# Splitting the first load by partitions and shortening the rows of the last loads in a nearest-neighbour upsampling kernel

## The chip, the cores and the metric

The kernel runs on one core of one Trainium2 chip. The metric is the device time of one execution, in microseconds (us), lower is better. A kernel was run several times, in rounds that alternate with the kernel before on the same chip. A span is the profiled part of one execution; it is about 1.8 us shorter than the time.

The work is done by DVE (VectorE) and ACT (ScalarE), which copy and replicate, and by the core's 16 DMA engines (16 packets are in flight at a time in the trace), which move data between HBM and the on-chip memory SBUF (tiles of 128 partitions). SP (SyncE) only issues the DMAs.

## The reference

```python
def setup_inputs():
    batch, channels, h, w = (16, 64, 64, 64)
    return {'x': np.random.randn(batch, channels, h, w).astype(np.float32), 'scale_factor': 2}

def reference(x, scale_factor):
    ...
    for i in range(new_h):          # 128
        for j in range(new_w):      # 128
            result[:, :, i, j] = x[:, :, i // scale_factor, j // scale_factor].copy()
    return result.astype(np.float32)
```

Every input value is written four times: 16.78 MB in, 67.11 MB out. There is no arithmetic.

## The kernel before

The rows of the input (65,536 rows of 64 values) are cut into eight loads of 2 MB. A load gives each of the 128 partitions 64 neighbouring rows, 16 KB in one piece. All eight are issued at once; the first is moved ahead of the barrier that ends the program's preamble. Then, for every half of a load, DVE replicates 18 rows of 32 and ACT the other 14 into a buffer `u` of 32 KB per partition, and a 4 MB store writes it out. There are two `u` buffers, so two stores can be in flight.

```python
def begin_before_barrier(nc):
    ...
    load = next(i for i in body.instructions if i.engine == sp)
    ...                                   # taken out of the body, put before SP's drain

    blocks = [64, 64, 64, 64, 64, 64, 64, 64]
    K = 32
    KV = 18
    ...
    upool = ctx.enter_context(tc.tile_pool(name="uexp", bufs=2))
    for n, k in enumerate(blocks):
        xt = xpool.tile([P, k, W], fdt, name=f"x{n}")
        nc.sync.dma_start(out=xt[:, :, :], in_=of_block(xf, first, k))
        ...
    for xt, first, k in loaded:
        for r0 in range(0, k, K):
            u = upool.tile([P, K, s, W, s], fdt, name="u")
            nc.vector.tensor_copy(out=u[:, :KV], in_=expanded(xt[:, r0 : r0 + KV, :]))
            nc.scalar.copy(out=u[:, KV:], in_=expanded(xt[:, r0 + KV : r0 + K, :]))
            nc.sync.dma_start(
                out=of_block(of, first, k)[:, r0 : r0 + K, :], in_=u[:, :, :, :, :])
```

Of the kernel before, what the change touches and what calls it, by code (L numbers as in the profile page):

```python
# [1 line left out]

# [4 lines left out]


def begin_before_barrier(nc):



    blocks = nc.main_func.blocks
    main, body = blocks[0], blocks[1]
    sp = mybir.EngineType.SP
    load = next(i for i in body.instructions if i.engine == sp)
    assert isinstance(load, mybir.InstDMACopy), type(load)
    assert not (load.sync_info and load.sync_info.on_wait)
    body.instructions = [i for i in body.instructions if i is not load]
    kept = list(main.instructions)  # L20
    at = next(
        n
        for n, i in enumerate(kept)
        if i.engine == sp and isinstance(i, mybir.InstDrain)
    )
    kept.insert(at, load)
    main.instructions = kept


@with_exitstack  # L30
def kernel(
    ctx: ExitStack,
    tc: tile.TileContext,
    x: bass.AP,
    scale_factor: int,
    out: bass.AP,
):
    nc = tc.nc
    nc.at_finalize(begin_before_barrier)
    P = nc.NUM_PARTITIONS  # L40
    s = int(scale_factor)
    B, C, H, W = x.shape
    R = B * C * H
    fdt = x.dtype



    blocks = [64, 64, 64, 64, 64, 64, 64, 64]

    K = 32  # L50
    assert P * sum(blocks) == R

    KV = 18

    xf = x.rearrange("b c h w -> (b c h) w")
    of = out.rearrange("b c (h hd) w -> (b c h) (hd w)", hd=s)

    def of_block(rows, first, k):
        return rows[first : first + P * k, :].rearrange("(p k) w -> p k w", p=P)

    xpool = ctx.enter_context(tc.tile_pool(name="xin", bufs=1))
    upool = ctx.enter_context(tc.tile_pool(name="uexp", bufs=2))

    loaded = []
    first = 0
    for n, k in enumerate(blocks):
        xt = xpool.tile([P, k, W], fdt, name=f"x{n}")
        nc.sync.dma_start(out=xt[:, :, :], in_=of_block(xf, first, k))
        loaded.append((xt, first, k))
        first += P * k  # L70

    def expanded(rows):
        return rows.unsqueeze(2).unsqueeze(4).to_broadcast(
            [P, rows.shape[1], s, W, s]
        )

    for xt, first, k in loaded:
        for r0 in range(0, k, K):
            u = upool.tile([P, K, s, W, s], fdt, name="u")
            nc.vector.tensor_copy(  # L80
                out=u[:, :KV], in_=expanded(xt[:, r0 : r0 + KV, :])
            )
            nc.scalar.copy(  # L83
                out=u[:, KV:], in_=expanded(xt[:, r0 + KV : r0 + K, :])
            )
            nc.sync.dma_start(
                out=of_block(of, first, k)[:, r0 : r0 + K, :],
                in_=u[:, :, :, :, :],
            )


# [1 line left out]
_INS = ['x', 'scale_factor']  # L93
_OUTS = [((16, 64, 128, 128), 'float32')]

_NUMBERS = {'scale_factor': 2}


# [26 lines left out]
```

## Time and profile before

| | before |
|---|---|
| time, median of 3 (range) | 199.86 us (199.73 to 199.90) |
| span | 198.0 us |
| busy: DMA queue, ACT, DVE | 99.0%, 26%, 21% |
| first data packet starts, after the first issue | 1.02 us |
| last data packet ends | 196.85 us |
| a 16 KB load packet, a 32 KB store packet | 611 ns, 1213 ns |

The last three rows are from the single DMA records of the trace, of which the views below are sums. One packet is one partition's piece of one DMA: 8 loads and 16 stores on 128 partitions leave 3072 data packets.

The page of the profile of the kernel before, its parts 1, 2 and 4. In part 2 the span is cut into 40 slices; "DMA" is the busy share in tenths, "GB/s" what was moved.

```profile
span 198.0 us, 149 instructions
...
DVE 40.9 (21%) x16; ACT 52.0 (26%) x17; POOL 0.2 (0%) x4
...
DMA  8999999999999999999999999999999999999995
GB/s 268 434 434 434 430 427 430 424 427 424 424 424 437 444 463 430 437 430 430 424 424 424 424 437 444 457 437 430 437 430 424 424 424 424 437 437 463 437 430 232
...
DMA 77%; ACT 14%; issue 0%; ACTq 0%
```

The DMA row is full from the second slice to the last but one, at 424 to 463 GB/s. The kernel is bound by the DMA engines. The ACT copies in the chain of part 4 are no second limit: while ACT and DVE fill one `u`, the other `u`'s store keeps the DMA engines busy (99.0% of the span).

The windows view of the same kernel, which the change is to alter: for each stretch its length, the busy time (and instructions) of DVE, ACT and POOL, the clock, the DMA share and GB/s. A packet is counted whole in the stretch where it starts, so a share can pass 1.

```profile
0.00:1.00 1.00, 0.00 (x0) 0.21 (x1) 0.20 (x4) 1.00 0.00 0
1.00:2.00 1.00, 0.00 (x0) 1.00 (x1) 0.00 (x0) 1.00 1.53 295
2.00:4.00 2.00, 0.00 (x0) 0.07 (x1) 0.00 (x0) 1.00 0.82 336
4.00:6.00 2.00, 0.00 (x0) 0.00 (x0) 0.00 (x0) 1.00 0.96 410
6.00:8.00 2.00, 0.15 (x1) 0.15 (x1) 0.00 (x0) 1.00 1.00 426
8.00:10.00 2.00, 2.00 (x1) 2.00 (x1) 0.00 (x0) 1.00 1.05 451
```

Nothing moves in the first microsecond, then the rate climbs, and from 4 us on it is 410 to 451 GB/s. This head is what the change goes for.

The waits view of the same kernel: who waited for what, in total us, times, longest us.

```profile
DVE u L80 <- DMA out_dram<-u: 131.8, 14, 39.3
...
DVE u L80 <- DMA x<-in_x_dram: 7.8, 1, 7.8
```

The second line gives the moment when the first 2 MB have landed: 7.8 us. It is not on the critical path (the first stores are issued at 11.1 and 14.1 us and then stand behind the other loads until about 40 us).

### The profile page before, as it was taken

To read this page: it belongs to the slowest core of one execution; us is meant where nothing else is said; L and a number is where in the kernel's file an instruction comes from. 1 tells how busy PE (TensorE), PEld (TensorE's weight loads), DVE (VectorE), ACT (ScalarE), POOL (GpSimd) and SP (SyncE) were. 2 spreads that over 40 slices of the span, in tenths; PEclk is the share of its full clock that TensorE was granted. 3 is DMA by queue.
4 is the path that set the end of the run, shared out by engine and by line. 5 is a ranking of instruction groups with operands and counts; after the bars stand their busy time and mean duration, and the time that the engine had idled before them with its cause. 6 is when DMAs were issued, how large, how long until landed. Compare 5 with 4: busy or idle time off the path is not lost.

```text
span 198.0 us, 149 instructions
## 1 busy us (share of the span) xinstructions
DVE 40.9 (21%) x16; ACT 52.0 (26%) x17; POOL 0.2 (0%) x4
## 2 busy tenths in 40 slices
DVE  0460000000405050505050505050505050504000
ACT  2480000000415150606060606060606060605000
POOL 0000000000000000000000000000000000000000
DMA  8999999999999999999999999999999999999995
GB/s 268 434 434 434 430 427 430 424 427 424 424 424 437 444 463 430 437 430 430 424 424 424 424 437 444 457 437 430 437 430 424 424 424 424 437 437 463 437 430 232
DMA packets 3456, 83.89 MB, mean 424 GB/s; under 512 B 384, under 2 KB 384, under 8 KB 384
## 3 DMA queue, kind: packets, MB, share of 16 engines
q1 hardware_dynamic: 3456, 83.89, 99.0%
HBM read 16.78 MB, written 67.11 MB: 424 GB/s over the span
## 4 chain that ended last, share of the span: by engine, by line
DMA 77%; ACT 14%; issue 0%; ACTq 0%
DMA out_dram<-u 73%; ACT u L83 14%; DMA x<-in_x_dram 4%; ACTq L83 0%
## 5 line engine op out<-in xcount | busy, mean ns | idle before, releaser
L83 ACT COPY u<-x 128x3584 f32<-128x3584 f32 x16 | 50.8, 3179 | 128.3 <-DMA out_dram<-u 122.5
L80 DVE COPY u<-x 128x4608 f32<-128x4608 f32 x16 | 40.9, 2560 | 139.7 <-DMA out_dram<-u 131.8
L83 ACT ACT_TABLE_LOAD x1 | 1.3, 1283 | 0.8 <-PEq L106 0.8
L106 POOL MEMSET const-bfloat16-1.0<- 128x1 bf16 x1 | 0.1, 102 | 0.0
L106 POOL MEMSET const-uint8-127<- 128x1 uint8 x1 | 0.1, 102 | 0.0
L106 POOL MEMSET const-float32-0.0<- 128x1 f32 x1 | 0.1, 98 | 0.2 <-issue 0.2
L106 POOL MEMSET const-float32-1.0<- 128x1 f32 x1 | 0.1, 98 | 0.0
## 6 DMA issues: line engine op xcount, KB each, us to landing
out_dram<-u SPq DMA_DIRECT2D x16, 4096.0 KB, 16.1
x<-in_x_dram SPq DMA_DIRECT2D x8, 2048.0 KB, 22.9
```

The source lines that it names most:

```text
L80: nc.vector.tensor_copy(out=u[:, :KV], in_=expanded(xt[:, r0 : r0 + KV, :]))
L83: nc.scalar.copy(out=u[:, KV:], in_=expanded(xt[:, r0 + KV : r0 + K, :]))
L106: nc = _bacc.Bacc("TRN2", target_bir_lowering=False, num_devices=1)
```

## The change

The intent, as the diff suggests: let the DMA engines start sooner by issuing first a small load with one packet for each of the 16 engines, issue the rest of the first load behind it before the barrier as well, keep the number of loads at eight by making one load of 4 MB, and use shorter rows (8 KB) where the loads end and the stores begin.

```diff
+EARLY = 2
...
-    load = next(i for i in body.instructions if i.engine == sp)
+    loads = [i for i in body.instructions if i.engine == sp][:EARLY]
...
-    blocks = [64, 64, 64, 64, 64, 64, 64, 64]
+    blocks = [(1, 64), (1, 64), (1, 128), (1, 64), (1, 64), (2, 32), (2, 32)]
...
-    for n, k in enumerate(blocks):
-        xt = xpool.tile([P, k, W], fdt, name=f"x{n}")
-        nc.sync.dma_start(out=xt[:, :, :], in_=of_block(xf, first, k))
+    for n, (j, m) in enumerate(blocks):
+        xt = xpool.tile([P, j, m, W], fdt, name=f"x{n}")
+        src = xf[first : first + j * P * m, :].rearrange(
+            "(j p m) w -> p j (m w)", j=j, p=P
+        )
+
+        for lo, hi in ((0, 16), (16, P)) if n == 0 else ((0, P),):
+            nc.sync.dma_start(out=xt[lo:hi], in_=src[lo:hi])
+        for jj in range(j):
+            parts.append((xt[:, jj], first + jj * P * m, m))
...
```

Copies and stores are the same, except that the last four stores each write 4 MB without gaps.

More of the change, by code (lines that the diff above doesn't have):

```diff
@@ L15, in begin_before_barrier @@
     sp = mybir.EngineType.SP
-    load = next(i for i in body.instructions if i.engine == sp)
-    assert isinstance(load, mybir.InstDMACopy), type(load)
-    assert not (load.sync_info and load.sync_info.on_wait)
-    body.instructions = [i for i in body.instructions if i is not load]
+    loads = [i for i in body.instructions if i.engine == sp][:EARLY]
+    for load in loads:
+        assert isinstance(load, mybir.InstDMACopy), type(load)
+        assert not (load.sync_info and load.sync_info.on_wait)
+    names = [i.name for i in loads]
+    body.instructions = [i for i in body.instructions if i.name not in names]
     kept = list(main.instructions)
@@ L25, in begin_before_barrier @@
     )
-    kept.insert(at, load)
+    kept[at:at] = loads
     main.instructions = kept
@@ L44 @@
     fdt = x.dtype
-    blocks = [64, 64, 64, 64, 64, 64, 64, 64]
+    blocks = [(1, 64), (1, 64), (1, 128), (1, 64), (1, 64), (2, 32), (2, 32)]
     K = 32
-    assert P * sum(blocks) == R
+    assert P * sum(j * m for j, m in blocks) == R
     KV = 18
@@ L56 @@
     of = out.rearrange("b c (h hd) w -> (b c h) (hd w)", hd=s)
-    def of_block(rows, first, k):
-        return rows[first : first + P * k, :].rearrange("(p k) w -> p k w", p=P)
     xpool = ctx.enter_context(tc.tile_pool(name="xin", bufs=1))
     upool = ctx.enter_context(tc.tile_pool(name="uexp", bufs=2))
-    loaded = []
+    parts = []
     first = 0
-    for n, k in enumerate(blocks):
-        xt = xpool.tile([P, k, W], fdt, name=f"x{n}")
-        nc.sync.dma_start(out=xt[:, :, :], in_=of_block(xf, first, k))
-        loaded.append((xt, first, k))
-        first += P * k
+    for n, (j, m) in enumerate(blocks):
[7 more added lines that the diff above has]
+            parts.append((xt[:, jj], first + jj * P * m, m))
+        first += j * P * m
     def expanded(rows):
@@ L75, in expanded @@
         )
-    for xt, first, k in loaded:
-        for r0 in range(0, k, K):
+    for xp, first, m in parts:
+        dst = of[first : first + P * m, :].rearrange("(p m) w -> p m w", p=P)
+        for r0 in range(0, m, K):
             u = upool.tile([P, K, s, W, s], fdt, name="u")
             nc.vector.tensor_copy(
-                out=u[:, :KV], in_=expanded(xt[:, r0 : r0 + KV, :])
+                out=u[:, :KV], in_=expanded(xp[:, r0 : r0 + KV, :])
             )
             nc.scalar.copy(
-                out=u[:, KV:], in_=expanded(xt[:, r0 + KV : r0 + K, :])
+                out=u[:, KV:], in_=expanded(xp[:, r0 + KV : r0 + K, :])
             )
             nc.sync.dma_start(
-                out=of_block(of, first, k)[:, r0 : r0 + K, :],
-                in_=u[:, :, :, :, :],
+                out=dst[:, r0 : r0 + K, :], in_=u[:, :, :, :, :]
             )
```

## The prediction

What it came to: 200.0 us, 80% range 199.2 to 202.8, where before took 199.86. It weighs a gain of 0.2 to 0.5 us (first packet 0.25 us earlier, 0.1 to 0.2 us given back where loads meet stores, 0.07 us for more packets taken off) against a loss of 1 to 4 us from the first load's split. Where a cut is marked, terms and conditions are gone: how the loss would come about, what the first packets would then take, and on what the earlier start depended. The 1 to 4 us and the 0.75 us are estimates.

> **What bounds the kernel now.** The DMA engines. The page has them 99.0% busy over the span of 198.0 us, moving 83.89 MB at 424 GB/s; DVE is busy 21%, ACT 26%. In the trace's DMA records the first data packet starts 1.02 us after the first issue and the last ends at 196.85 us; between them 16 packets are in flight, so there is no hole. A 16 KB load packet takes 611 ns, a 32 KB store packet 1213 ns. Chained end to start, packets form 16 streams of 192 packets and 5.24 MB. 128 x 1213 + 64 x 611 ns is 194.4 us per engine. Only the rest can be saved: 1.0 us before the first packet; about 0.9 us per engine because the first packets take 768 to 1914 ns; about 0.45 us between 38 and 41 us, where last loads and first stores meet; 0.7 us of skew among the engines' ends; 1.2 us from the last packet to the span's end. Compute is hidden: the chain of waits shows copies, but the stores issued at 11.1 and 14.1 us queue behind loads until 40 us, and later copies (3.2 us) run under the other store.
>
> **What the change does.**
> - Same bytes, copies, sixteen stores and eight loads.
> - The first load becomes 16 + 112 partitions, both issued ahead of the barrier. [...] its start moves from 1.0 to about 0.75 us. Issuing the second early fills no hole, as there is none. SP reaches the barrier some 0.4 us later, which delays only ACT and DVE, with 5 us to spare.
> - Packets: 128 of 32 KB replace 256 of 16 KB, 512 of 8 KB replace another 256. From 611 and 1213 ns a packet's fixed part is 9 ns, so this costs about 0.07 us per engine (estimate). Smaller packets where loads meet stores may give back 0.1 to 0.2 of the 0.45 us.
> - The last four stores write 4 MB contiguously instead of at 64 KB pitch. Stores already run at 1213 ns flat: no gain.
>
> **The risk.** [...] An engine behind at the start stays behind, because nothing later is idle. [...] The trace of before can't show this: all its transfers have 128 partitions.
>
> **Prediction.** Gain of 0.2 to 0.5 us [...], loss of 1 to 4 us [...]. I put it at 200.0 us, 80% range 199.2 to 202.8; faster by over 2% 0.01, within 2% 0.94, slower by over 2% 0.05.
>
> **What would show it.** First packet near 0.75 us after the first issue; duration of the first 16 packets [...] and of the 112-partition load's against 611 ns; the excess at 38 to 41 us below 0.45 us; 16 active packets throughout; stores still 1213 ns; the skew of the engines' ends.
>
> **What would make it wrong.** The 112-partition load spread over fewer engines or very unevenly (loss over 4 us), or a start delay that a smaller load doesn't shorten (no gain).

## The result, and the profile after

| | before | after |
|---|---|---|
| time, median (range), 4 runs each (one more of before) | 199.88 us (199.73 to 200.00) | 202.71 us (202.50 to 202.87) |
| span | 198.0 us | 200.8 us |
| first data packet starts | 1.02 us | 1.02 us |
| first 2 MB landed (waits view) | 7.8 us | 11.3 us |
| last data packet ends | 196.85 us | 199.69 us |

The ratio is 1.0139, with a 95% interval of 1.0124 to 1.0154. A ratio is the mean time of one kernel's fast runs over that of the other's of the same rounds, so not quite the ratio of the medians quoted. The changed kernel is 2.8 us slower: within 2%, but far outside the noise.

The page of the changed kernel, its parts 1, 2, 4 and 6 (part 6: what each DMA moves, and its time from issue to landing).

```profile
span 200.8 us, 153 instructions
...
DVE 40.9 (20%) x16; ACT 52.0 (26%) x17; POOL 0.2 (0%) x4
...
DMA  8999899999999999999999999999999999999995
GB/s 170 297 427 450 379 427 419 423 454 418 431 470 444 431 418 418 418 450 476 418 431 418 418 424 450 470 431 418 418 418 431 457 457 431 418 418 418 444 463 241
...
DMA 76%; ACT 15%; issue 0%; SPq 0%; ACTq 0%
...
x<-in_x_dram SPq DMA_DIRECT2D x1, 1792.0 KB, 10.7
x<-in_x_dram SPq DMA_DIRECT2D x1, 256.0 KB, 4.3
```

The DMA row is as full as before, but the GB/s row is not: the first two slices moved at 170 and 297 GB/s where the kernel before had 268 and 434. Busy and moving are different things. The first piece, an eighth of the first load, took 4.3 us to land. (That alone says little: 256 KB on all 128 partitions took 3.9 us in e4_rowsplit, below.)

The windows view of the changed kernel, the same stretches and one more:

```profile
0.00:1.00 1.00, 0.00 (x0) 0.00 (x0) 0.20 (x4) 1.00 0.00 0
1.00:2.00 1.00, 0.00 (x0) 0.00 (x0) 0.00 (x0) 1.00 1.82 328
2.00:4.00 2.00, 0.00 (x0) 0.00 (x0) 0.00 (x0) 1.00 0.69 123
4.00:6.00 2.00, 0.00 (x0) 0.00 (x0) 0.00 (x0) 1.00 0.97 262
6.00:8.00 2.00, 0.00 (x0) 0.00 (x0) 0.00 (x0) 1.00 1.22 352
8.00:10.00 2.00, 0.00 (x0) 0.00 (x0) 0.00 (x0) 1.00 1.01 270
...
12.00:16.00 4.00, 4.00 (x2) 3.99 (x3) 0.00 (x0) 1.00 0.99 422
```

From 2 to 10 us, with the engines marked busy, the core moves 123 to 352 GB/s; from 12 us on it is back to 422. In the DMA records the first 16 packets take 1.31 us on average (1.38 in the kernel before, nearly the same), the 16 behind them 1.68 us, four of these 2.03 to 2.06 us, and the packets that start from 3.8 to 9.3 us about 985 ns (median) instead of 611. All this time 16 packets are in flight, as in the kernel before: no engine is missing, each is slower.

To say what such slow packets cost I use one number below, the *extra packet time*: every packet's duration less the usual one for its size (611 ns for 16 KB, 1213 ns for 32 KB, and for other sizes the straight line through these two, which is 9 ns plus 37.6 ns per KB), summed and divided by the 16 engines. The queue never runs dry (16 packets in flight), so an engine that loses time early should end later by that much; the sum below, 3.0 us, and the later end of the last packet, 2.84 us, bear this out.

| extra packet time per engine | before | after |
|---|---|---|
| start, packets from 0 to 20 us | 0.94 us | 4.19 us |
| where loads meet stores, 36 to 50 us | 0.47 us | 0.12 us |
| everything else | 0.05 us | 0.10 us |

The start costs 3.25 us more, the meeting of loads and stores 0.35 us less, the rest 0.05 us more; 128 more packets at 9 ns over 16 engines are 0.07 us. The sum, about 3.0 us, matches the last packet's 2.84 us later end; the engines' ends differ a little less than before. Each of these figures is from one profiled execution. e7_store below runs the same loads as the kernel before and has 0.84 and 0.34 us in the first two rows instead of 0.94 and 0.47, so a difference of about 0.1 us here is no finding.

The timeline of the changed kernel (start us, us, engine, line, operation, and what ended the idle time before it) shows what follows: the first copies wait longer, and ACT's table load, which stood at 0.79 us before, now stands behind the wait for the first load.

```profile
11.23 1.28 ACT L94 ACT_TABLE_LOAD   x1 [11.23 <-DMA x<-in_x_dram]
11.25 5.03 DVE L91 COPY u<-x 128x4608 f32<-128x4608 f32 x2 [11.25 <-DMA x<-in_x_dram]
...
15.73 3.44 SPq L97 DMA_DIRECT2D out_dram<-u  x2
```

The first store is issued at 15.7 us rather than 11.1, but the loads keep the engines busy beyond 40 us, so this costs nothing. The question is why packets are slow from 2 to 10 us.

### The profile page after: what moved, and what is told of

Read it like the earlier page. It is cut to its first block, busy times and chain, and to the rows that moved or that the text cites. A ratio compares the mean times of both kernels' runs of the same rounds, so it can differ in the third digit from the quotient of the medians.

```text
span 200.8 us, 153 instructions
## 1 busy us (share of the span) xinstructions
DVE 40.9 (20%) x16; ACT 52.0 (26%) x17; POOL 0.2 (0%) x4
## 4 chain that ended last, share of the span: by engine, by line
DMA 76%; ACT 15%; issue 0%; SPq 0%; ACTq 0%
DMA out_dram<-u 71%; ACT u L94 14%; DMA x<-in_x_dram 5%; ACT L94 1%; SPq L77 0%; ACTq L94 0%
## 5 line engine op out<-in xcount | busy, mean ns | idle before, releaser
L94 ACT ACT_TABLE_LOAD x1 | 1.3, 1283 | 11.2 <-DMA x<-in_x_dram 11.2
```

The source lines that it names most:

```text
L94: nc.scalar.copy(out=u[:, KV:], in_=expanded(xp[:, r0 + KV : r0 + K, :]))
```

## The experiments

**Theory (width).** The partitions that a DMA covers set the rate at which its packets move, whatever it reads in HBM: a DMA on fewer than all 128 moves more slowly. The traces of before and after alone don't show this, and the half and the quarter of the rate in the expectations of e3 and e13 were the author's assumption. What the expectations said of its cause is cut: no trace or run shows it. Where a cut is marked before the first figures of an expectation, these are what this theory forecasts. **Rivals.** (a) Two loads ahead of the barrier disturb the start. (b) Any cut of the load costs a fixed time. (c) The loss belongs to the cold start. (d) The engines clash in HBM addresses. (e) Seven rows per engine (112 packets, 16 in flight at a time), an uneven number, is the harm, or the 16 partitions standing first. (f) The 8 KB rows.

Twelve kernels were run; the times of before in the three sets were 199.84, 199.72 and 199.97 us (medians of 9). Each set ran on a chip of its own, so a kernel is compared with before of its own set. All results were correct but one.

| label | what it is | time, us (median, range) | ratio to before (95%) | extra packet time at start / where loads meet stores, us |
|---|---|---|---|---|
| e1_nosplit | changed, first load whole | 199.90 (199.60 to 200.31) | 1.0006 (0.9994 to 1.0019) | 0.98 / 0.28 |
| e2_norows | changed, 16 KB rows | 202.59 (202.31 to 202.91) | 1.0138 (1.0124 to 1.0152) | 4.18 / 0.06 |
| e3_halves | changed, 64 + 64 | 204.05 (203.97 to 204.37) | 1.0214 (1.0200 to 1.0228) | 5.22 / 0.13 |
| e4_rowsplit | changed, cut along the rows | 200.26 (200.02 to 200.55) | 1.0022 (1.0008 to 1.0035) | 1.16 / 0.29 |
| e5_mid | 16 + 112 in the fourth load | 204.32 (203.92 to 204.56) | 1.0227 (1.0213 to 1.0241) | 0.88, and 4.40 at 20 to 36 us / 0.06 |
| e6_pitch | as e3, other HBM addresses | 204.22 (204.05 to 204.35) | 1.0226 (1.0211 to 1.0242) | 5.20 / 0.13 |
| e7_store | before, one store 64 + 64 | 209.99 (209.57 to 210.19) | 1.0510 (1.0496 to 1.0525) | 0.84, and 9.31 past 50 us / 0.34 |
| e8_128 | before, four loads of 4 MB | 200.05 (200.01 to 200.68) | 1.0022 (1.0009 to 1.0034) | 0.75 / 0.88 |
| e10_mixed | candidate, nothing split | 200.00 (199.86 to 200.17) | 1.0003 (0.9990 to 1.0015) | 0.59 / 0.72 |
| e11_rows | before, 8 KB rows alone | 199.89 (199.59 to 200.08) | 0.9996 (0.9983 to 1.0008) | 0.79 / 0.14 |
| e12_last16 | changed, 112 + 16 | 204.00 (203.66 to 204.50) | 1.0201 (1.0181 to 1.0222) | 4.59 / 0.12 |
| e13_sixteens | changed, eight pieces of 16 | 211.61 (211.51 to 211.89) | 1.0586 (1.0572 to 1.0600) | 12.80 / 0.12 |

### Is it the split? (e1_nosplit, e2_norows, e4_rowsplit)

```diff
-        for lo, hi in ((0, 16), (16, P)) if n == 0 else ((0, P),):
+        for lo, hi in ((0, P),):
```

> The changed kernel with its first load whole again (128 partitions); the two early issues and the 8 KB rows stay. [...] the 3.2 us of extra packet time in the first 10 us goes, 199.4 to 199.7 us. Rival (two loads ahead of the barrier disturb the start): stays near 202.7 us.

Measured 199.90 us, level with before, and the extra packet time at the start is back at 0.98 us. The windows view of this kernel has the rate of before again:

```profile
4.00:6.00 2.00, 0.00 (x0) 0.00 (x0) 0.00 (x0) 1.00 1.04 442
6.00:8.00 2.00, 0.00 (x0) 0.00 (x0) 0.00 (x0) 1.00 0.98 418
8.00:10.00 2.00, 1.93 (x1) 1.93 (x1) 0.00 (x0) 1.00 1.01 434
```

The whole loss comes from the split; two whole loads ahead of the barrier do no harm. Rival (a) is out.

```diff
-    blocks = [(1, 64), (1, 64), (1, 128), (1, 64), (1, 64), (2, 32), (2, 32)]
+    blocks = [(1, 64), (1, 64), (1, 128), (1, 64), (1, 64), (1, 64), (1, 64)]
```

> The changed kernel with the last two loads as 16 KB rows again. The trace of the changed kernel has about 0.1 us of packet excess where loads meet stores, that of before 0.46 us; if the 8 KB rows are the reason, this kernel shows the 0.4 us again and takes 202.9 to 203.1 us. If the rows do nothing but add packets, 202.6 us.

Measured 202.59 us, no slower than with the 8 KB rows. My expectation was wrong: the smaller extra where loads meet stores (0.06 us) is there without the 8 KB rows too. So the rows are not needed for it here (they may do it too: e11_rows, below, has 0.14 us with these rows and no split). Rival (f) is out.

```diff
-        for lo, hi in ((0, 16), (16, P)) if n == 0 else ((0, P),):
-            nc.sync.dma_start(out=xt[lo:hi], in_=src[lo:hi])
+        for lo, hi in ((0, 8), (8, m)) if n == 0 else ((0, m),):
+            nc.sync.dma_start(
+                out=xt[:, :, lo:hi, :].rearrange("p j m w -> p j (m w)"),
+                in_=src[:, :, lo * W : hi * W],
+            )
```

> The changed kernel with the first load split by its rows, 8 of 64 and 56 of 64 on all 128 partitions, instead of by partitions. [...] 199.4 to 199.7 us. Rival (splitting the first load, or two loads queued early, costs by itself): 202.7 us. First packet at 1.0 us if the start delay is fixed, earlier if it depends on the bytes of the load.

Measured 200.26 us: the same first load in two DMAs, the first of the same 256 KB, but each on all 128 partitions. The 3.25 us are gone, so a cut as such costs no such time, and rival (b) is out as an explanation. It is still 0.2% above before and a little above what I expected, and it gains nothing: its first packet, of only 2 KB, also starts at 1.02 us.

### Does the loss follow the width? (e3_halves, e12_last16, e13_sixteens)

```diff
-        for lo, hi in ((0, 16), (16, P)) if n == 0 else ((0, P),):
+        for lo, hi in ((0, 64), (64, P)) if n == 0 else ((0, P),):
```

> The changed kernel with the first load split 64 + 64 instead of 16 + 112. [...] the 2 MB run at half rate, about 4.8 us lost, 204.2 us and 16 KB packets of about 1.2 us for the first ten us. Rival (seven rows per engine, an uneven number, is what hurts) : 199.5 us. Rival (any second load in the first place costs a fixed time): 202.7 us, as 16 + 112.

Measured 204.05 us, worse than 16 + 112, as of these only the width theory says: an even number of rows per engine doesn't help. The 16 KB packets from 2.5 to 10 us take 1280 ns (median), 2.1 times 611. The windows view of this kernel:

```profile
2.00:4.00 2.00, 0.00 (x0) 0.00 (x0) 0.00 (x0) 1.00 1.21 262
4.00:6.00 2.00, 0.00 (x0) 0.00 (x0) 0.00 (x0) 1.00 0.87 180
6.00:8.00 2.00, 0.00 (x0) 0.00 (x0) 0.00 (x0) 1.00 1.00 213
8.00:10.00 2.00, 0.00 (x0) 0.00 (x0) 0.00 (x0) 1.00 1.20 246
```

About half of the 410 to 451 GB/s that the kernel before has from 4 to 10 us.

```diff
-        for lo, hi in ((0, 16), (16, P)) if n == 0 else ((0, P),):
+        for lo, hi in ((0, 112), (112, P)) if n == 0 else ((0, P),):
```

> The changed kernel with the 16 partitions last: 112 + 16 instead of 16 + 112. [...] a loss of 2 to 3 us over before stays, 201.7 to 202.9 us. Rival (the harm is done by the 16 partitions standing first, which set the engines out of step): about 200 us.

Measured 204.00 us. The loss doesn't need the 16 partitions to stand first, so that half of rival (e) is out; but it is 4.0 us, more than I expected, and more than with the 16 first. Of the 1.3 us between the two orders only 0.4 us is packet time (4.59 against 4.19 us); the rest is that the engines' last packets end 2.0 us apart instead of 0.55. I come back to this with e5.

```diff
-        for lo, hi in ((0, 16), (16, P)) if n == 0 else ((0, P),):
+        for lo, hi in [(q, q + 16) for q in range(0, P, 16)] if n == 0 else ((0, P),):
```

> The changed kernel with its first load in eight pieces of 16 partitions. [...] the first 2 MB move at about a quarter of the rate, 105 to 115 GB/s, and take about 19 us instead of 4.9: 211 to 214.5 us. [...] Rival (a fixed cost per cut): rate unchanged between the pieces.

Measured 211.61 us, inside what was expected. The windows view of this kernel:

```profile
2.00:4.00 2.00, 0.00 (x0) 0.00 (x0) 0.00 (x0) 1.00 1.11 131
4.00:6.00 2.00, 0.00 (x0) 0.00 (x0) 0.00 (x0) 1.00 1.05 123
6.00:8.00 2.00, 0.00 (x0) 0.00 (x0) 0.00 (x0) 1.00 1.12 131
8.00:10.00 2.00, 0.00 (x0) 0.00 (x0) 0.00 (x0) 1.00 1.13 131
10.00:12.00 2.00, 0.00 (x0) 0.00 (x0) 0.00 (x0) 1.00 1.13 131
12.00:16.00 4.00, 0.00 (x0) 0.00 (x0) 0.00 (x0) 1.00 0.95 111
```

Sixteen packets of 16 KB go in step, 2216 ns each from 5 to 16 us: 16 x 16,384 B in 2.216 us is 118 GB/s, a little over a quarter of the full rate. The first 2 MB land at 19.9 us:

```profile
DVE u L91 <- DMA x<-in_x_dram: 19.9, 1, 19.9
```

So the rate steps down with the width of the DMA: 128 partitions about 430 GB/s, 64 about half (180 to 262 in e3), 16 about a quarter (118 in e13). It is not in proportion to the width, for 16 partitions are an eighth of it. Nor are engines missing: 16 packets are in flight throughout in both kernels. What makes the steps was not shown.

### SBUF or HBM, start or middle? (e6_pitch, e5_mid, e7_store)

```diff
 # e3_halves, and:
+        if n == 0:
+            src = xf[: 2 * P * m, :].rearrange("(p t m) w -> p t (m w)", t=2, m=m)
+            src = src[:, 0:1, :]
```

> The 64 + 64 split of e3_halves, but every partition of the first load reads its 16 KB at a pitch of 32 KB in HBM (wrong result on purpose)[...]. [...] unchanged, 204.1 us. Rival (the engines clash in HBM addresses[...]): clearly different from 204.1, by a microsecond or more.

The result is wrong (half of what the first load reads are other rows than its own). Measured 204.22 us, and 5.20 us of extra packet time at the start against 5.22 in e3_halves. Doubling the pitch in HBM changes nothing, which speaks against rival (d). It is one other set of addresses, not all of them.

```diff
 # the changed kernel, and:
-EARLY = 2
+EARLY = 1
-    blocks = [(1, 64), (1, 64), (1, 128), (1, 64), (1, 64), (2, 32), (2, 32)]
+    blocks = [(1, 64), (1, 64), (1, 128), (1, 64), (1, 64), (1, 64), (1, 64)]
-        for lo, hi in ((0, 16), (16, P)) if n == 0 else ((0, P),):
+        for lo, hi in ((0, 16), (16, P)) if n == 3 else ((0, P),):
```

> The 16 + 112 split moved from the first load to the fourth (16 KB rows, one early issue), so nothing about the start differs from before. [...] the same loss as in the changed kernel, about 2.8 us, 202.6 us, with slow packets near 20 to 28 us instead of 2 to 10. Rival (the loss belongs to the start of the kernel, with cold memory and the table load): 199.8 us.

Measured 204.32 us. The loss moves with the split, so rival (c) is out, and it is larger: 4.6 us against 2.8. The windows view of this kernel shows the start undisturbed and the slow stretch at 22 to 32 us:

```profile
10.00:20.00 10.00, 2.87 (x2) 4.10 (x2) 0.00 (x0) 1.00 1.00 429
...
22.00:24.00 2.00, 0.00 (x0) 0.00 (x0) 0.00 (x0) 1.00 0.76 115
24.00:26.00 2.00, 0.00 (x0) 0.00 (x0) 0.00 (x0) 1.00 0.93 262
26.00:28.00 2.00, 0.00 (x0) 0.00 (x0) 0.00 (x0) 1.00 0.99 270
28.00:30.00 2.00, 0.00 (x0) 0.00 (x0) 0.00 (x0) 1.00 0.96 262
```

The split costs 4.40 us of extra packet time here; at the start of the changed kernel the whole head, split and all, has 4.19 us, of which 0.94 us was there before. A likely reading, not tested by itself: at the start the slow first packets (768 to 1914 ns in the kernel before too) and the slow packets of the split overlap in time, so less is added. In e12_last16, where the 16 partitions come second, the head has 4.59 us.

```diff
 # the kernel before, and:
+            half = first == 4 * P * k and r0 == 0
+            for lo, hi in ((0, 64), (64, P)) if half else ((0, P),):
                 nc.sync.dma_start(
-                    out=of_block(of, first, k)[:, r0 : r0 + K, :],
-                    in_=u[:, :, :, :, :],
+                    out=of_block(of, first, k)[lo:hi, r0 : r0 + K, :],
+                    in_=u[lo:hi, :, :, :, :],
                 )
```

> The kernel before, with one store of 4 MB in the middle split into 64 + 64 partitions. [...] that store runs at half rate, packets of about 2.4 us instead of 1.21, and the time rises by about 9 to 9.6 us to 209 us. If only writes into SBUF clash: 199.9 us.

Measured 209.99 us, 10.3 us over before, for one store of sixteen cut in halves. A store of 4 MB takes 8 x 1213 ns = 9.7 us at full rate, so half rate adds 9.7 us. In packet time it is 9.31 us per engine; the engines' ends also lie further apart (1.9 us, 0.7 before). The direction is the other one, the cost the same in kind: 180 to 279 GB/s while the halves move, 434 after. For the store no kernel with other HBM addresses was run. The windows view of this kernel:

```profile
110.00:118.00 8.00, 2.56 (x1) 3.18 (x1) 0.00 (x0) 1.00 1.04 451
118.00:122.00 4.00, 1.91 (x1) 1.93 (x1) 0.00 (x0) 1.00 0.98 279
122.00:126.00 4.00, 0.66 (x1) 1.25 (x1) 0.00 (x0) 1.00 1.27 262
126.00:130.00 4.00, 0.00 (x0) 0.00 (x0) 0.00 (x0) 1.00 0.79 197
130.00:134.00 4.00, 0.00 (x0) 0.00 (x0) 0.00 (x0) 1.00 1.13 229
134.00:138.00 4.00, 0.00 (x0) 0.00 (x0) 0.00 (x0) 1.00 0.78 180
138.00:142.00 4.00, 2.25 (x1) 2.27 (x1) 0.00 (x0) 1.00 1.02 434
```

### Is there a version that beats both? (e8_128, e11_rows, e10_mixed)

```diff
-    blocks = [64, 64, 64, 64, 64, 64, 64, 64]
+    blocks = [128, 128, 128, 128]
```

> The kernel before with four loads of 4 MB (32 KB rows) instead of eight of 2 MB. From 611 and 1213 ns a packet's fixed part is 9 ns; 32 packets per engine fewer save 0.29 us: 199.55 us. The first store is issued later (about 18 us) but still behind the queued loads, so it costs nothing. If the fixed part is not real: 199.85 us. If the late first store matters: over 200 us.

Measured 200.05 us, 0.2% over before: a miss. The packets are fewer, but the extra where loads meet stores rose from 0.47 to 0.88 us and took the gain back: the last packet ends at 196.85 us in both. Where the 0.3 us more comes from is open.

```diff
 # changed, not split, EARLY = 1
-    blocks = [(1, 64), (1, 64), (1, 128), (1, 64), (1, 64), (2, 32), (2, 32)]
+    blocks = [(1, 64)] * 6 + [(2, 32), (2, 32)]
```

> The kernel before with the 8 KB rows alone (last two loads), nothing split, one early issue. Sixteen more packets per engine cost 0.14 us, the excess where loads meet stores falls by 0.2 us: 199.7 us, no difference that can be told from before.

Measured 199.89 us where before took 199.97: no difference, as expected. This is the change without its split and its second early issue; I see no more in the change to gain.

```diff
 # changed, not split, EARLY = 1
-    blocks = [(1, 64), (1, 64), (1, 128), (1, 64), (1, 64), (2, 32), (2, 32)]
+    blocks = [(1, 128), (1, 128), (1, 128), (1, 64), (2, 32)]
```

> Candidate to beat both: whole 128-partition loads, three of 4 MB (32 KB rows), one of 2 MB, and only the last in two 8 KB rows; one early issue. Estimate from the traces: 16 packets per engine fewer than before at 9 ns each save 0.14 us, and the excess where loads meet stores falls from 0.46 us (16 KB rows) to about 0.26 (8 KB rows, e1_nosplit): 199.4 to 199.5 us where before takes 199.75. Rival (these small terms do not reach the total): 199.75 us.

Measured 200.00 us where before took 199.97: the rival. The extra where loads meet stores was 0.72 us here with 8 KB rows, against 0.14 (e11) and 0.28 (e1), where the last two loads have these rows. The rows of the last load alone do not set this term. What does is open, as is why it is nearly gone (0.06 to 0.13 us) in every kernel with a load split by partitions. No version that I ran beats the kernel before.

## Why the prediction was right or wrong

The time, 202.71 us, lies in the predicted range of 199.2 to 202.8, but 0.09 us from its upper end, and the middle of the prediction (200.0 us) leaned to the wrong side. That it fell inside is partly luck: the same 16 + 112 split takes 204.32 us in the fourth load (e5) and 204.00 us in the other order (e12), both outside. That the split loses time held (2.8 us). Point by point:

- **"What bounds the kernel now. The DMA engines."** Right. What changed the time was DMA time alone; a first copy at 11.3 us instead of 7.8 and a table load pushed to 11.2 us cost nothing.
- **"its start moves from 1.0 to about 0.75 us".** Wrong. The first packet starts at 1.02 us with 16 partitions first as with 128, at 1.01 us with 112 (e12), at 1.02 us with 2 KB rows (e4), and at 0.99 us with 32 KB rows (e8). The start delay does not shrink with the load. This was the gain that the change is built on; where no load is split by partitions (e1, e4, e11) there is none of the predicted 0.2 to 0.5 us.
- **"Issuing the second early fills no hole".** Right: e1_nosplit is level with before (199.90 against 199.84 us).
- **"this costs about 0.07 us per engine" and "may give back 0.1 to 0.2 of the 0.45 us".** The first is too small to be told in the time. The second came out at 0.35 us, but the small packets are not its proven reason: e2_norows has it with 16 KB rows and the split, e11_rows has it with 8 KB rows and no split.
- **"Stores already run at 1213 ns flat: no gain".** Right, 1213 ns after too.
- **"The risk".** How the loss would come about, the runs don't show. What they show is that the partitions that a DMA covers set the rate, in steps (half for 64 in e3, a quarter for 16 in e13), not the cut (e4), the place in the program (e5), or the one other HBM pitch tried (e6). The size, "loss of 1 to 4 us", held: 3.25 us of extra packet time, 2.8 us in the time. The "duration of the first 16 packets" was no test: they took 1.31 us, 1.38 in the kernel before; the delay showed in the packets behind them (four took over 2 us). The sixteen records end by 2.83 us, the 256 KB landed at 4.3 us. So here the end of a packet record was no proof that its data had landed. "16 active packets throughout" held.
- **The weighing.** The range left room for the loss (202.8 us), the middle (200.0 us) did not. The trace of before could not weigh it, as all its transfers have 128 partitions.

**What stays open.** The trace doesn't name the engine of a packet, so which partitions each engine gets in a 112-partition load was not seen. Why DMAs with few partitions are slow was not shown either; that their width is the cause rests on the steps of the rate (a half in e3, a quarter in e13), and no load of 64 partitions other than 0 to 63 and 64 to 127 was run. Without this the cost of 16 + 112 can't be worked out beforehand from these runs: it was 2.8 us at the start and 4.6 us in the fourth load. And in the two kernels whose first load had 64 partitions (e3, e6) the first packet started later, at 1.32 us against 0.99 to 1.05 in the others; why is open too.

## What to carry to other kernels

Cut a transfer along the free dimension, not along the partitions, when the DMA engines are the limit: here 64 + 64 partitions cost 4.2 us on a 2 MB load and 10.3 us on a 4 MB store, while the load cut along its rows (8 + 56 of 64) cost 0.4 us. A DMA row that is full says only that packets are in flight (8 and 9 tenths in the first two slices of the changed kernel, at 123 to 352 GB/s from 2 to 10 us); read the GB/s beside it and the packet durations before calling an engine well used. And check that the delay that a change is to shorten depends on what the change shrinks: the first packet came about 1.0 us after its issue whether the load had 256 KB or 4 MB (1.3 us in e3 and e6).
